# Nine late experts of 128 places, normed at a token's second visit, beside the tiles of the other tokens

## The chip, the core and the metric

One core of a Trainium2 chip. The time is that of the device for one execution of the whole kernel, in microseconds (us). PE is the matrix engine, DVE the vector engine, ACT the scalar engine, POOL the GpSimd engine (it also issues all DMAs with row lists), SP the engine that issues the weight loads.

## The reference, cut to what matters

One residual block over 2048 tokens of 1024 numbers. A mixer (convolution and gated DeltaNet) is added to x first. Then comes a mixture of experts, and the last norm:

```python
h = rms_norm(x, ffn_norm_g)
x = x + hier_moe(h, router_group_w, router_expert_w, w_gate, w_up, w_down)
return rms_norm(x, final_norm_g)
```

The router picks one of 4 groups for a token and 2 of the group's 8 experts; an expert is `(silu(x @ w_gate) * (x @ w_up)) @ w_down` with 1024, 512 and 1024 columns. So there are 4096 visits of a token to an expert, 32 experts, and a token's output row can be normed when both of its experts have been added.

On the inputs that the reference draws, the router sends between 85 and 173 tokens to an expert. With the experts ordered as the kernel does it, the last 3 get 300 visits by 288 tokens; the last 9 get 1002 visits by 842 tokens, of which 160 come twice; 1206 tokens come to none of the nine. The number of tokens whose first of two late visits is at the first, second, ... ninth late expert: 37, 40, 31, 0, 14, 26, 12, 0, 0.

## The kernel before, in words

Up to about 1060 us the mixer runs; then the block's sums x are written to `acc_d` in memory, and the normed halves of h to `h2_d`. Routing gives each expert a rank: ranks 0 to 2 are experts picked early, which had few tokens in the first half; the rest follow by falling number of tokens. `CAPS` (L725) gives each rank a number of places. Lists of token numbers, one per place, stand in `tabG` (for gathers, always a valid row), `tabS` (for scatters; an empty place points past the last row and is skipped) and `gix` (for the gates).

Each expert is one `Job` of one chunk (up to 128 places) or two. The loop at L1488 runs the 32 jobs; its first half (`gate_up`, 192 matmuls whose moving side has one column per place) and second half (`down`) are each woven by `weave` with other generators, which hand out the places in program order; from there the tile framework sets the order on each engine and the waits. For one job there are:
- `load_part` (L766, L775): 12 stages of 512 KB, loaded by SP into `mst` tiles, scaled and split into two f16 halves by ACT (`wgu`, `wd`, L92) and DVE (L93). `stage()` takes the tiles from two pools of five in turn. The split halves have two buffers each, so the next expert is loaded while one runs. SP's queue runs in order.
- `fetch` (L1050, L1055): POOL gathers the tokens' rows of h and their gates; `turn` (L1066, L1067) turns them on PE.
- `gate_up` (L1081 to L1088), then `down`. With one chunk, `down` makes 24 matmuls of 512 columns (L1116) and ACT scales by the gate (L1125). With two chunks, it makes 96 matmuls with one column per place (L1151), and PE turns the result back (L1138, L1142).
- `add` (L1094): POOL scatters the result onto `acc_d`, adding in memory, one DMA for each chunk.

The order of jobs (L1329 on) takes large and small ranks in turn: 2, 28, 3, 27, 4, 26, ..., 16, 15, and then the last three ranks, 29 to 31 (`LAST = 3`). All tiles of tokens are normed at the end: `others` (L1252) makes the list `bix`, by which a tile's tokens with a visit to the last three are left out. The first eight tiles are gathered into stages (`load_early`, L1378) when the last weights are through, the other eight (`load_late`) into a weight buffer after the last gathers. `norm_all` squares (L1366), takes the root (L1369, a power on POOL at L1370), applies the gain (L1373) and writes twelve tiles by SP as whole tiles (L1410) and four by lists on POOL (L1414). Rows of the late tokens are gathered once more (`rows_of`, L1421), normed (`norm_rows`) and scattered last (`store_rows`, L1432); the last expert's result is added to gathered sums on DVE (L1123) rather than in memory. `behind` and `issue_after` hold the norms back behind the experts' work. A loop for experts with more tokens than places follows; it runs no round on these inputs.

## Time and profile before

| what | us |
|---|---|
| median of 3 runs | 1954.14 (1949.02 to 1956.95) |
| the profiled execution | 1948.9 |
| its span | 1947.1 |
| PE busy | 1752.6 |
| DVE busy | 1403.5 |
| ACT busy | 1007.2 |
| POOL busy | 426.7 |

Times in the trace count from the start of the span. "Busy" of PE is modelled, as matmuls overlap. The DMA share is the mean over the core's 16 DMA engines of the time that packets took, so it can come out a little over 1. A `POOL DMA_INDIRECT` row is the time that POOL takes to issue a DMA with a row list; its data land later. In a timeline row the brackets name the idle time before the instruction and what ended it.

### The profile page before, as it was taken

To read this page: it belongs to the slowest core of one execution; us is meant where nothing else is said; L and a number is where in the kernel's file an instruction comes from. 1 tells how busy PE (TensorE), PEld (TensorE's weight loads), DVE (VectorE), ACT (ScalarE), POOL (GpSimd) and SP (SyncE) were. 2 spreads that over 40 slices of the span, in tenths; PEclk is the share of its full clock that TensorE was granted. 3 is DMA by queue.
4 is the path that set the end of the run, shared out by engine and by line. 5 is a ranking of instruction groups with operands and counts; after the bars stand their busy time and mean duration, and the time that the engine had idled before them with its cause. 6 is when DMAs were issued, how large, how long until landed. Compare 5 with 4: busy or idle time off the path is not lost.

```text
span 1947.1 us, 41829 instructions
## 1 busy us (share of the span) xinstructions
PE 1752.6 (90%) x16221; PEld 1199.0 (62%) x16221; DVE 1403.5 (72%) x2713; ACT 1007.2 (52%) x1676; POOL 426.7 (22%) x375
## 2 busy tenths in 40 slices
PE   6789999999999999999999969999899999999840
PEld 5455555555555554444454438888788899999730
DVE  8889888888888745322344768777778888888732
ACT  5655434444444424211233637766667767777621
POOL 1321111121111100000000013223322344344343
PEclk9889999999999999999999979999999999999975
DMA  4122001001001105002255967999999999999873
GB/s 143 67 69 53 11 15 46 16 13 46 20 11 37 36 19 165 28 12 60 98 175 189 346 233 258 334 308 306 303 320 359 354 335 340 351 341 317 285 225 142
DMA packets 203597, 330.27 MB, mean 170 GB/s; under 512 B 44590, under 2 KB 98935, under 8 KB 203394
## 3 DMA queue, kind: packets, MB, share of 16 engines
q1 hardware_dynamic: 178738, 271.20, 40.9%
q0 software_dynamic: 20128, 47.30, 9.5%
q10 hardware_dynamic: 4528, 9.06, 1.2%
q8 instruction: 129, 2.11, 0.4%
q14 instruction: 74, 0.61, 0.1%
HBM read 276.05 MB, written 54.82 MB: 170 GB/s over the span
## 4 chain that ended last, share of the span: by engine, by line
PE 29%; DMA 20%; DVE 8%; issue 5%; ACT 5%; POOL 1%; SPq 1%; ACTq 0%; DVEq 0%; POOLq 0%
PE acc L134 11%; DMA mst<-in_w_up_dram 10%; PE a L1081 8%; DMA mst<-in_w_down_dram 5%; PE a L988 5%; DMA mst<-in_w_gate_dram 3%; DVE wgu L93 3%; ACT wgu L92 2%; DVE wd L93 1%; PE pn L548 1%; DMA end<-acc_d,tabG 1%; ACT yo L1142 1%; DMA mst<-acc_d,bix 1%; PE pl L1138 1%; SPq L766 1%
## 5 line engine op out<-in xcount | busy, mean ns | idle before, releaser
L134 PE MATMUL acc<-hT,whl 128*128 128x512 f16 x2640 | 635.3, 381 | 0.2 <-DVE hT L203 0.2
L134 PEld LDWEIGHTS <-whl 128*128 128x128 f16 x2640 | 252.9, 99 | 248.4 <-issue 11.4
L1081 PE MATMUL a<-xT,wgu 128*128 128x128 f16 (+17 forms) x6144 | 394.7, 227 | 3.3 <-DVE sl L1088 2.4
L1081 PEld LDWEIGHTS <-wgu 128*128 128x128 f16 x6144 | 389.3, 99 | 9.5 <-issue 3.5
L93 DVE SCALAR_TENSOR_TENSOR wgu<-mst,gw,wgu 128x1024 f16<-128x1024 f32 x256 | 317.5, 1276 | 19.9 <-ACT wgu L92 17.6
L92 ACT ACTIVATE wgu<-mst,gw 128x1024 f16<-128x1024 f32 x256 | 280.8, 1139 | 36.0 <-DMA mst<-in_w_up_dram 33.7
L988 PE MATMUL a<-wo,yb 128*128 128x512 f16 x768 | 176.3, 381 | 0.0
L93 DVE SCALAR_TENSOR_TENSOR wd<-mst,wd 128x1024 f16<-128x1024 f32 x128 | 154.2, 1215 | 3.6 <-ACT wd L92 3.5
L1094 POOL DMA_INDIRECT acc_d<-yo,tabS x50 | 95.9, 1918 | 265.9 <-ACT yo L1142 191.8
L92 ACT ACTIVATE wd<-mst 128x1024 f16<-128x1024 f32 x128 | 131.3, 1047 | 24.3 <-DMA mst<-in_w_down_dram 24.1
L1151 PE MATMUL a<-ac,wd 128*128 128x144 f16 (+12 forms) x1824 | 136.9, 230 | 4.9 <-ACT ac L92 3.9
L1151 PEld LDWEIGHTS <-wd 128*128 128x128 f16 x1824 | 124.4, 98 | 8.3 <-issue 6.5
L988 PEld LDWEIGHTS <-yb 128*128 128x128 f16 x768 | 72.2, 98 | 79.6 <-issue 3.0
L294 DVE SCALAR_TENSOR_TENSOR cv<-raw,pcol,cv 128x512 f32<-128x512 f32 x144 | 117.1, 815 | 1.6
L1050 POOL DMA_INDIRECT xr<-h_d,tabG x51 | 61.5, 1206 | 179.2 <-PE t L1066 159.0
L1088 DVE SCALAR_TENSOR_TENSOR sl<-a,sl 128x128 f32<-128x128 f32 (+17 forms) x128 | 38.3, 300 | 78.1 <-ACT sl L1087 77.6
L1087 ACT ACTIVATE sl<-a 128x128 f32<-128x128 f32 (+17 forms) x128 | 35.7, 280 | 108.9 <-PE a L1081 108.9
L1116 PE MATMUL pl<-wd,ac 128*128 128x512 f16 (+4 forms) x312 | 78.6, 397 | 6.1 <-ACT ac L92 4.8
L382 DVE TENSOR_TENSOR pr<-Ts,fs 32x1 f32<-32x1 f32 (+14 forms) x240 | 76.6, 319 | 4.4 <-DMA fs<-dscr 0.7
L1055 POOL DMA_INDIRECT gs<-gt_d,gix x51 | 74.3, 1457 | 15.7 <-issue 15.4
L545 ACT ACTIVATE osq<-acv 128x512 f32<-128x512 f32 x16 | 10.1, 628 | 125.3 <-DVE acv L543 125.3
L1138 PE MATMUL pl<-id,yt 128*128 128x128 f32 (+13 forms) x304 | 52.8, 292 | 23.4 <-ACT yo L1142 17.2
(357 smaller groups left out, 2536.6 us busy)
## 6 DMA issues: line engine op xcount, KB each, us to landing
mst<-in_w_gate_dram SPq DMA_DIRECT2D x256, 256.0 KB
mst<-in_w_up_dram SPq DMA_DIRECT2D x256, 256.0 KB
mst<-in_w_down_dram SPq DMA_DIRECT2D x128, 512.0 KB
wst<-in_w_in_dram SPq DMA_DIRECT2D x28, 512.0 KB
xt<-in_x_dram SPq DMA_DIRECT2D x16, 512.0 KB
ydr<-yh SPq DMA_DIRECT2D x64, 128.0 KB
x<-in_x_dram SPq DMA_DIRECT2D x16, 512.0 KB
yb<-ydr SPq DMA_DIRECT2D x16, 512.0 KB
```

What stands on the lines that cost most here:

```text
L92: A.activation(hi, src, AF.Copy, scale=scale)
L93: (eng or V).scalar_tensor_tensor(lo, src, scale, hi, op0=OP.mult, op1=OP.subtract)
L134: T.matmul(acc, w[:, i, k, :], hT[b][:, j, k, :], start=(n == 0), stop=(n == 3 * KT - 1))
L294: V.scalar_tensor_tensor(y, tap(j), pcol[:, q:q + 1], y, op0=OP.mult, op1=OP.add)
L382: V.tensor_tensor(q, Ts[:, 0:i, 0:i].rearrange("p j m -> p m j"), bc(fs[:, None, 0:i, i], [32, i, i]), op=OP.mult)
L988: T.matmul(po, yb[:, i, k, c * P:(c + 1) * P], wo[:, j, k, n * FF:(n + 1) * FF], start=(q == 0), stop=(q == 3 * KT - 1))
L1055: G.indirect_dma_start(out=g[0:cw], out_offset=None, in_=gt_d[0:end * NE, :], in_offset=IO(ap=gx, axis=0))
L1081: T.matmul(pg[:, q, 0:n], wq[:, i, k, q, f * P:(f + 1) * P], xT[:, j, k, 0:n], start=(z == 0), stop=(z == 3 * KT - 1))
L1094: st = G.indirect_dma_start(out=acc_d, out_offset=IO(ap=sx, axis=0), in_=yo[0:cw], in_offset=None, bounds_check=S - 1, oob_is_err=False, c ...
L1116: T.matmul(py[0:n], ac[:, i, k, 0:n], wd[:, j, k, q * FF:(q + 1) * FF], start=(z == 0), stop=(z == 3 * FF // P - 1))
L1138: T.transpose(py[0:cw, c * P:(c + 1) * P], yts[d2][:, u, off:off + cw], id32)
L1151: T.matmul(pg[:, u, 0:n], wd[:, i, k, d * P:(d + 1) * P], ac[:, j, k, 0:n], start=(z == 0), stop=(z == 3 * FF // P - 1))
```

## The change

- `LAST` is 9, so ranks 23 to 31 come last, with 128 places each (112 for the last). The jobs before them are then rank 2 (128 places), 22 (128), 3 (216), 21 (136), 4 (192), 20 (136), 5 (176), 19 (136), 6 (176), 18 (136), 7 (168), 17 (136), 8 (160), 16 (144), 9 (160), 15 (144), 10 (152), 14 (144), 11 (152), 13 (144), 12 (152).
- Places are rounded up to multiples of 8, and gathers (`even`) to multiples of 16 rows.
- `others` and the new `visits` make two lists per late expert: `tabF` (tokens whose first of two late visits this is) and `tabL` (tokens whose last visit this is), through a table `fl_d` in memory.
- In each of the late jobs but the last, the sums of the job's tokens are gathered to `so` at the start of `down` (`sums_before`). Its result is scattered onto `acc_d` for the tokens of `tabF` alone (`first_sums`). In the next job DVE adds result and sums, and the rows are normed and scattered to the output by `tabL` (`second_sums`).
- In each of the first eight late jobs two tiles of the other tokens are gathered into two stages during `gate_up` and normed and scattered to the output by `bix` during `down` (`load_tiles`, `norm_tiles`); no tile is written by SP.
- The last job ends with its own norm and scatter alone. The tables of routing move into tiles that other tables have left.

```diff
-    CAPS = [C1, C1, C1, 216, 188, 176, 172, 164, 160, 156, 152, 148, 148, 144, 144, 144, 140, 136, 136, 136,
-            132, 132, 128, 128, 124, 124, 124, 120, 120, 120, 116, 112]
+    CAPS = [C1, C1, C1, 216, 192, 176, 176, 168, 160, 160, 152, 152, 152, 144, 144, 144, 144, 136, 136, 136,
+            136, 136, 128, 128, 128, 128, 128, 128, 128, 128, 128, 112]
-    LAST = 3
+    LAST = 9
...
+    def even(n):
+        return max(n, min(-(-n // 16) * 16, CM - P if n <= CM - P else P))
...
     def others():
-        pq = o1.tile([P, 2, NT, NE], F32, name="pq2", tag="hx", bufs=1)
-        V.tensor_tensor(pq, OH, bc(last[:, None, None, :], [P, 2, NT, NE]), op=OP.mult)
-        yield 1
-        m = o2.tile([P, 2, NT], F32, name="om", bufs=1)
-        V.tensor_reduce(m, pq, axis=AX, op=OP.add)
...
+        for i, row in ((0, last), (1, capE)):
+            pq = o1.tile([P, 2, NT, NE], F32, name="pq2", tag="hx", bufs=1)
+            V.tensor_tensor(pq, OH, bc(row[:, None, None, :], [P, 2, NT, NE]), op=OP.mult)
+            yield 1
+            V.tensor_reduce(m[:, i], pq, axis=AX, op=OP.add)
+            yield 1
...
+        V.scalar_tensor_tensor(fl[:, :, 0], m[:, 2, 0], -BIG, tok, op0=OP.mult, op1=OP.add)
+        V.scalar_tensor_tensor(fl[:, :, 1], m[:, 2, 1], BIG, tok, op0=OP.mult, op1=OP.add)
+        nc.gpsimd.dma_start(fl_d.rearrange("(t p) c -> p t c", p=P), fl)
...
+    def visits():
+        for l in range(LAST):
+            G.indirect_dma_start(out=flp[:, l], out_offset=None, in_=fl_d,
+                                 in_offset=IO(ap=tabG[:, NE - LAST + l, 0:1], axis=0))
+            yield 1
...
-    AHEAD = 8
-    LP, WE = 0, 0.6
-    GT = 4
-    NPL = NT - GT
+    GT = 2
...
+    def load_tiles(t0):
+        for t in range(t0, t0 + GT):
             xs[t] = stage()
-            load(t)
+            st = G.indirect_dma_start(out=xs[t], out_offset=None, in_=acc_d,
+                                      in_offset=IO(ap=bix[:, t:t + 1], axis=0), bounds_check=S - 1,
+                                      oob_is_err=False)
...
-    def load_late():
...
-    def norm_all():
...
+    def norm_tiles(t0):
+        s = o2.tile([P, GT], F32, name="ss4")
+        for i in range(GT):
+            square(xs[t0 + i], s[:, i:i + 1])
+            yield 1
+        root(s)
+        yield 1
+        for i in range(GT):
+            x = xs.pop(t0 + i)
+            gain(x, s[:, i:i + 1])
+            store_rows(x, bix[:, t0 + i:t0 + i + 1])
+            yield 1
...
-    def finish(J):
...
+    def first_sums(J, l):
+        st = G.indirect_dma_start(out=acc_d, out_offset=IO(ap=tabF[0:J.n, l:l + 1], axis=0),
+                                  in_=(J.base or J.yo)[0][0:J.n], in_offset=None, bounds_check=S - 1,
+                                  oob_is_err=False, compute_op=OP.bypass if J.base else OP.add)
...
+    def sums_before(J):
+        J.so = rows_of(J.chunks[0][0], J.n, m2.tile([P, D], F32, name="so", bufs=1))
+        yield 1
+
+    def second_sums(J, l):
+        n, x = J.n, J.so
+        V.tensor_tensor(x, x, J.yo[0][0:n], op=OP.add)
+        yield 1
+        s = o2.tile([P, 1], F32, name="ss1", bufs=4)[0:n]
+        square(x, s, n)
+        yield 1
+        root(s)
+        yield 1
+        gain(x, s, n)
+        store_rows(x, tabL[0:n, l:l + 1])
+        yield 1
...
+        if l > 0:
+            parts.append((second_sums(jobs[j - 1], l - 1), 4, 0.1, 0.6))
+        if tl is not None:
+            parts.append((load_tiles(tl), GT, 0.5, 0.7))
+        if left == 1:
             J.base = [rows_of(J.chunks[0][0], J.n, stage())]
-            ends = [(rows_of(L.chunks[0][0], L.n, o1.tile([P, D], F32, name="end", tag="hh")), L.chunks[0][2])
-                    for L in jobs[-LAST:-1]]
-            load_late()
...
+        parts = [(part(j + 2, 0), 4, 0, 1)]
+        if 0 <= l and left > 1:
+            parts.append((sums_before(J), 1, 0, 0.1))
+        if tl is not None:
+            parts.append((norm_tiles(tl), 2 * GT + 1, 0, 0.9))
...
     end = stage()[0:J.n]
-    def rest():
-        for x, sx in ends:
-            norm_rows(x)
-        yield from slices(na, 2 * GT)
-        norm_rows(J.base[0][0:J.n], end)
-        yield from slices(na, 2 * GT)
-        for x, sx in ends + [(end, J.chunks[0][2])]:
-            store_rows(x, sx)
-    drain(behind(rest(), marks[-1]))
+    norm_rows(J.base[0][0:J.n], end)
+    store_rows(end, tabL[0:J.n, LAST - 1:LAST])
+    drain(first_sums(J, LAST - 1))
```

## Rows read from the trace of the kernel before

**Rows 1.** Busy us (instructions) by stretch; last: PE clock, DMA share, GB/s.

```profile
core 0: us, PE busy (x) PEld busy (x) DVE busy (x) ACT busy (x) POOL busy (x), PEclk, DMA share, GB/s
1700.00:1800.00 100.00, 98.45 (x1532) 94.40 (x1530) 87.89 (x126) 76.19 (x111) 42.97 (x27) 1.00 1.02 332
...
1850.00:1900.00 50.00, 23.95 (x240) 16.46 (x240) 14.93 (x28) 14.91 (x35) 20.96 (x21) 0.77 0.75 231
1900.00:1947.00 47.00, 0.00 (x0) 0.00 (x0) 13.66 (x14) 7.87 (x16) 13.59 (x12) 0.50 0.36 135
```

**Rows 2.** Timeline of PE, first `gate_up` matmuls of jobs 4, 5, 6, 17, 23, 31.

```profile
1241.63 17.92 PE L1081 MATMUL a<-xT,wgu 128*128 128x216 f16 x192
...
1272.55 0.90 PE L1081 MATMUL a<-xT,wgu 128*128 128x120 f16 x14
...
1290.14 15.68 PE L1081 MATMUL a<-xT,wgu 128*128 128x188 f16 x192
...
1550.39 0.39 PE L1081 MATMUL a<-xT,wgu 128*128 128x132 f16 x4
...
1682.07 0.58 PE L1081 MATMUL a<-xT,wgu 128*128 128x136 f16 x7
...
1860.28 0.85 PE L1081 MATMUL a<-xT,wgu 128*128 128x112 f16 x14
```

**Rows 3.** POOL's groups, from 1600 us on: busy us, mean ns, idle before.

```profile
L1094 POOL DMA_INDIRECT acc_d<-yo,tabS x19 | 35.7, 1880 | 70.5 <-ACT yo L1142 67.4 <-ACT sl L1087 1.5 <-issue 0.9
L1055 POOL DMA_INDIRECT gs<-gt_d,gix x19 | 30.0, 1577 | 5.8 <-issue 5.8
L1050 POOL DMA_INDIRECT xr<-h_d,tabG x18 | 22.5, 1248 | 35.3 <-PE t L1066 35.3
...
L1378 POOL DMA_INDIRECT mst<-acc_d,bix x8 | 15.5, 1936 | 15.3 <-DMA mst<-in_w_down_dram 13.1 <-DVE wgu L93 0.6 <-issue 0.6
...
L1414 POOL DMA_INDIRECT out_dram<-xw,bix x4 | 5.8, 1452 | 2.5 <-DVE xw L1373 1.9 <-issue 0.6
L1370 POOL TENSOR_TENSOR ss<-ss,mhalf 128x4 f32<-128x4 f32 x4 | 5.0, 1247 | 9.0 <-DVE ss L1369 9.0
```

**Rows 4.** Two stretches of one us: weights alone; gates and adds beside them.

```profile
1663.00:1664.00 1.00, 1.00 (x19) 1.00 (x17) 1.00 (x2) 1.00 (x2) 1.00 (x1) 1.00 1.07 406
...
1690.00:1691.00 1.00, 1.00 (x21) 1.00 (x19) 1.00 (x3) 0.32 (x1) 1.00 (x1) 1.00 1.02 234
```

**Rows 5.** DMA of 1500 to 1600 us.

```profile
DMA packets 15583, 35.31 MB, mean 353 GB/s; under 512 B 2124, under 2 KB 2124, under 8 KB 15568
```

**Rows 6.** DVE's groups by shape, from 1600 us on.

```profile
L93 DVE SCALAR_TENSOR_TENSOR wgu<-mst,gw,wgu 128x1024 f16<-128x1024 f32 x72 | 89.6, 1275 | 0.0
L93 DVE SCALAR_TENSOR_TENSOR wd<-mst,wd 128x1024 f16<-128x1024 f32 x38 | 46.1, 1213 | 0.0
L1067 DVE COPY xT<-t 128x1024 f16<-128x1024 f16 x18 | 11.5, 680 | 0.0
...
L93 DVE SCALAR_TENSOR_TENSOR ac<-sl,ac 128x136 f16<-128x136 f32 x12 | 3.5, 293 | 1.1 <-ACT ac L92 1.1
...
L1373 DVE SCALAR_TENSOR_TENSOR mst<-mst,ss,gfin 128x1024 f32<-128x1024 f32 x8 | 10.0, 1277 | 5.2 <-POOL ss L1370 5.2
```

**Rows 7.** Timeline of POOL and DVE in the tail.

```profile
1865.40 2.17 POOL L1094 DMA_INDIRECT acc_d<-yo,tabS  x1 [8.81 <-ACT sl L1087]
...
1879.32 1.02 POOL L1421 DMA_INDIRECT mst<-acc_d,tabG  x1 [10.67 <-DMA acc_d<-yo,tabS]
...
1936.64 0.96 POOL L1432 DMA_INDIRECT out_dram<-mst,tabS  x1 [8.51 <-DMA out_dram<-end,tabS]
...
1887.18 1.41 DVE L1123 SCALAR_TENSOR_TENSOR mst<-pl,gs,mst 112x512 f32<-112x512 f32 x2 [11.43 <-DMA mst<-acc_d,tabG]
```

**Rows 8.** Us from issue to landing after 1800 us; SP's waits (sum, times, longest), 1600 to 1800.

```profile
mst<-acc_d,bix POOLq DMA_INDIRECT x8, 7.1
...
SPq L775 <- DVE wgu L93: 38.5, 11, 5.7
```

**Rows 9.** Timeline of POOL, a gather of a tile while DVE splits weights.

```profile
1840.44 6.60 POOL L1378 DMA_INDIRECT mst<-acc_d,bix  x1 [0.31 <-DVE wgu L93]
```

## What the change will do to the time

> **What bounds the kernel now.** I read the stretches first (busy time, granted clock and DMA by stage), then the matrix engine's starts by job, then what every engine does in one job, then the chain of waits at the end. The second part of the kernel runs 32 experts ("jobs"). In the steady part DMA is always busy and PE, DVE and ACT are at 98, 88 and 76 of 100 us; after the last weights have landed, DMA falls to a share of 0.36 and PE stands still with its clock at half [rows 1]. So there are two regimes: a middle where nothing has much room, and a tail of 86.8 us, from the start of the last job (1860.28) to the end of the span (1947.1), in which the sums of all tokens are read back, normed and written. The change takes work out of the tail and puts it into the full stretch; the question is what it costs there.
>
> What one job takes is seen where successive jobs start [rows 2]. The six two-chunk jobs from 1550.39 to 1682.07 took 131.7 us for 848 places, 21.95 each at 141.3 places. A place more costs 192 + 96 matmul columns, 0.12 us at the full clock of 2.4 GHz, so 21.3 us at 136 places; the job of 216 then comes to 30.9, and 30.92 is what it took (1241.63 to 1272.55). A one-chunk job has no transposes back and took 17.6 (to 1290.14): it leaves PE room, and there DMA sets the pace.
>
> **The middle.** Before, jobs 4 to 22 alternate large and small experts and took 440.4 us (1241.63 to 1682.07) [rows 2]. After, the small experts are kept for the end, and the same 19 jobs are all two-chunk, with 2960 places: 19 x 21.3 + (2960 - 2584) x 0.12 = 450 us by PE. DMA needs 6.29 MB of weights and 156 places x 8 KB, 7.6 MB in 23.7 us, 320 GB/s, under the 332 that a hundred steady microseconds held [rows 1]; so PE is the bound. The rounded places are in this sum (36 places here, 4.3 us); the extra rows that a gather brings for 16 (at most 8 a job) are DMA alone and hidden. In jobs 4 and 5 come the tables: the nine gathers of `visits` have no counterpart, the nearest is the gather of gates, 1.58 us of POOL each [rows 3], while the DMA rate falls from 406 to 234 GB/s in such stretches [rows 4]: 14 us x 0.42 = 6 us of DMA as the upper end, none as the lower, since those jobs are PE-bound. The store of 2048 eight-byte pieces and the DVE work of `others` lie beside a 31 us job. I take 4: the middle is 13.6 us longer. Ends: +9.6, and +21 with the 6 us and 1 us more in each of the five jobs of 136 places (7.4 MB at 332 GB/s is 22.3 us, not 21.3).
>
> **The nine late jobs.** Each of eight jobs gets: 128 sums gathered, two tiles gathered (1206 tokens in 16 tiles, so 151 rows), three norms, 151 rows and (from the second) some 94 scattered to the output; its scatter-add shrinks from some 110 rows to 18. What each resource needs for one such job:
> - DMA: 6.29 weights + 0.52 for tokens + 0.52 sums + 0.62 + 0.62 tiles + 0.38 second visits + 0.07 first sums = 9.02 MB. At 353 GB/s, the best hundred microseconds [rows 5], 25.6 us; at 332 [rows 1], 27.2. For the higher rate speaks that the add in memory, which runs where the rate is down at 234 [rows 4], is nearly gone.
> - DVE: 8 x 1.24 + 4 x 1.21 splits, 2 x 0.64, 8 x 0.29 (`ac`, and `sl` of the same shape), three gains at 1.25, an add (not shown before at this place; its operands are as large as the gain's, so 1.25, with 0.64, the copy of half the bytes, and 2.5, the gain twice, as ends), roots 0.3: 23.7 us, busy time by count [rows 6].
> - POOL, which also takes over the twelve tile stores that SP issues now: 1.25 + 1.58 for the fetch, 3 x 1.94 gathers of sums, 3 x 1.45 stores, 1.88 for the first sums, two powers at 1.25, and 0.3 between instructions: 20.7 us [rows 3].
> - PE 18; three squares go into ACT's room.
>
> So DMA sets 25.6 us; I take it, as the fraction of adds is the larger difference between the two rates. The first of them lacks the second visit: 24.4. Jobs 23 to 30 take 24.4 + 7 x 25.6 = 203.6, against 178.2 before (1682.07 to 1860.28) [rows 2]: 25.4 longer. Ends: 23.7 a job (DVE) and 30 (below). The PE clock may fall in the waits, as to 0.77 late now [rows 1]; with 18 of 25.6 us it has cover, and none if jobs became PE-bound.
>
> **The tail.** Now: the last job starts at 1860.28, the scatter-add before it is issued at 1865.40, the gather of its sums waits for that until 1879.32, DVE has them at 1887.18, and then come twelve more tiles, norms, and three scatters in a row to 1936.64 [rows 7]. After: the same chain without the tiles. The scatter-add of job 30 has no row left (no token of it has a later visit), so its landing is short: gather at about +11 from the job's start, landed at +18, as gate_up (192 x 112 columns at 2.4 GHz, 9.0) and 24 matmuls of 512 columns at 0.21 end at about +16 with their waits; two evictions 1.5, square, root, power, gain 4, issue and landing 5, and the end of the program 5 to 6, as after the last issue now [rows 7]. That is 34 us against 86.8: 52.8 shorter. Ends: 30, and 50 if the wait for the add stays as it is now (10.7 us) and the last second visit stands before the last norm on DVE and POOL.
>
> **The sum.** 13.6 + 25.4 - 52.8 = -13.8. The profiled execution took 1948.9 (span 1947.1), so 1935.1; it stands 5.2 under the median of 1954.1, so the forecast is 1940, 0.7% faster. About 0.5%, 9.8 us, is what a measurement of this kernel can tell from no change.
>
> **Rivals.**
> - **DMA is not the limit, DVE is.** Gathers of whole rows may run near the 406 GB/s of the weights [rows 4]; then a late job takes DVE's 23.7: 15 us less, 1925. For it: no add in memory. Against: every steady hundred microseconds stayed at 332 to 353. Chance 0.22.
> - **The stage buffers run out (slower).** The tiles are gathered into the ten stages through which the weights pass. A tile holds its stage from its gather (7.1 us to landing [rows 8]) over squares, power and gains to the landing of its store, some 21 us, while that buffer comes round again after 10 of 14 stages, 18 us. The next weight load is issued late, and all loads behind it on SP's queue with it, where SP already waits up to 5.7 us for stages [rows 8]. Behind it on ACT and DVE stands the split, and behind that the activations of the running expert. Price: nothing to 10 us a job; with the doubled weight buffers hiding a little over half, 4.4: 30 us a job, 1971. It decides against the change above 27.6 us a job, by over 0.5% above 29. Chance 0.20.
> - **POOL becomes the bound.** One gather of a tile took 6.60 us while DVE ran splits without a pause, where its like take 1.94 [rows 3, 9]. Eight of POOL's eleven instructions in a late job are such issues beside a DVE that is nearly full. If one and a half a job go that way, 7 us more: 27.7 a job, 1955. Chance 0.12. The Trainium skill (SBUF — State Buffer, section "Who interferes with whom") says that a DVE instruction with two inputs from SBUF contends with a GpSimd instruction that reads SBUF, under an exclusive lock, and so speaks against this change; the trace agrees in that one row, not in the others, and were it the rule each time, the sum would be this rival's.
> - **The tail does not shrink as meant**, 50 us for 34: 1956. Chance 0.06.
>
> **How the numbers follow.** The forecast has 0.40; its own range, 24.7 to 27 us a job, is 1932 to 1950. Of that 0.28 lies under 1944.4. Faster by over 0.5%: 0.28 + 0.22 = 0.50. Within 0.5%: 0.12 + 0.10 (POOL) + 0.05 (tail) = 0.27. Slower: 0.20 + 0.03 = 0.23. The range leaves out the lower part of the second case and the upper half of the stage rival: 1914 to 1972.
>
> **What would show it.** Job starts: nineteen jobs from 1241 to about 1696, eight about 25 us apart, the last at 1900, the end 34 us later. In the late stretch DMA share near 1.0 at about 350 GB/s, DVE over 90 of 100, POOL near 80. If the wait rows of SP show the landing of a store to the output or of a tile as releaser, with DMA share under 0.9, the stages were the limit. If POOL has no idle time and long issues, POOL was. If the middle is longer than 462, the reading that PE bounds it is wrong. Late jobs under 23 us would show DVE's sum as too large.

## The result, and the profile after

The changed kernel takes 1980.2 us (median of 4 runs, 1969.4 to 1981.2), the kernel before 1951.6 beside it: a ratio of 1.0133, 95% interval 1.0087 to 1.018. It is slower by 1.3%, where 0.7% faster was forecast, and lies above the range. The profiled execution of the change took 1981.2, its span is 1979.1, 32.0 longer than the 1947.1 of before.

First the timeline of PE: the first `gate_up` matmuls of jobs 1, 4, 23 and 31 in the changed kernel ([rows 2] for before).

```profile
1202.16 2.03 PE L1088 MATMUL a<-xT,wgu 128*128 128x128 f16 x29
...
1261.10 3.12 PE L1088 MATMUL a<-xT,wgu 128*128 128x216 f16 x32
...
1715.91 0.50 PE L1088 MATMUL a<-xT,wgu 128*128 128x128 f16 x6
...
1948.87 7.88 PE L1088 MATMUL a<-xT,wgu 128*128 128x112 f16 x157
```

The starts split the 32.0 us into the terms of the forecast:

| stretch | before | after | difference | forecast |
|---|---|---|---|---|
| up to job 4 | 1241.6 | 1261.1 | +19.5 | 0 |
| jobs 4 to 22 | 440.4 | 454.8 | +14.4 | +13.6 |
| jobs 23 to 30 | 178.2 | 233.0 | +54.8 | +25.4 |
| job 31 to the end | 86.8 | 30.2 | -56.6 | -52.8 |

Two terms hold. One of 19.5 us was not in the sum, and the late jobs take 29.1 us each (233.0 / 8) for 25.5 in the sum (203.6 / 8). The profiled execution is the slowest of the change's four, so the table splits 32.0 us, where the medians differ by 28.6. The tail is as described: POOL's and DVE's timeline of the changed kernel has the gather of the last sums, the add of the second half, and the last scatter (answering to [rows 7]).

```profile
1955.53 0.96 POOL L1448 DMA_INDIRECT mst<-acc_d,tabG  x1 [0.30 <-issue]
...
1968.50 0.97 POOL L1413 DMA_INDIRECT out_dram<-mst,tabL  x1 [1.61 <-DVEq L1558]
...
1964.13 0.75 DVE L1130 SCALAR_TENSOR_TENSOR mst<-pl,gs,mst 112x512 f32<-112x512 f32 x1 [1.84 <-PE pl L1123]
```

Now the stretches of the changed kernel, to be held against [rows 1] (busy time of each engine, PE clock, DMA share, GB/s).

```profile
core 0: us, PE busy (x) PEld busy (x) DVE busy (x) ACT busy (x) POOL busy (x), PEclk, DMA share, GB/s
1700.00:1800.00 100.00, 74.23 (x919) 59.53 (x917) 66.84 (x90) 60.76 (x92) 45.12 (x33) 0.88 0.84 271
1850.00:1900.00 50.00, 35.39 (x383) 24.38 (x384) 35.27 (x46) 33.05 (x48) 19.37 (x15) 0.83 0.90 312
1950.00:1979.00 29.00, 13.83 (x197) 11.32 (x194) 9.36 (x17) 4.32 (x12) 9.48 (x9) 0.80 0.21 67
```

In the late stretch nothing is full: DMA has a share of 0.84 to 0.90 at 271 to 312 GB/s, DVE 67 of 100, POOL 45. So neither the forecast's limit nor that of the rivals on DVE and POOL was reached; the time is in waits. The view of waits of the changed kernel, 1745 to 1945 (sum, times, longest):

```profile
POOL so L1448 <- DMA out_dram<-so,tabL: 43.4, 7, 7.8
...
ACT wgu L92 <- DMA mst<-in_w_up_dram: 25.4, 23, 3.5
ACT wd L92 <- DMA mst<-in_w_down_dram: 21.8, 13, 3.8
PE a L1088 <- DVE sl L1095: 19.2, 6, 8.9
...
DVE mst L1410 <- POOL ss L1407: 14.0, 6, 7.3
...
SPq L776 <- DMA out_dram<-mst,bix: 58.1, 6, 14.0
...
SPq L767 <- DMA out_dram<-mst,bix: 5.3, 1, 5.3
```

SP waits 63 us until a tile's scatter to the output has landed and a stage is free, and ACT 47 us for the weights that come late; [rows 8] had at most 5.7 us at a time, for a stage that DVE was still splitting. That is the row named ahead for the stage rival, with its 30 us a job. But POOL waits too. How one wait can make the next is seen in one timeline, from the second half of job 24 into job 25 (POOL, DVE, SP, PE, in this order); of the eight late jobs it is the one with the longest waits before the power and the gain:

```profile
1765.61 0.94 POOL L1448 DMA_INDIRECT so<-acc_d,tabG  x1 [4.39 <-DMA out_dram<-so,tabL]
1774.75 1.61 POOL L1460 DMA_INDIRECT acc_d<-yo,tabF  x1 [8.20 <-DMA so<-acc_d,tabG]
1775.83 1.29 POOL L1407 TENSOR_TENSOR ss<-ss,mhalf 128x2 f32<-128x2 f32 x1
...
1782.02 2.03 POOL L1413 DMA_INDIRECT out_dram<-mst,bix  x1 [0.30 <-DVE wgu L93]
...
1768.48 0.16 DVE L1406 TENSOR_SCALAR ss<-ss 128x2 f32<-128x2 f32 x1
...
1777.15 2.48 DVE L1410 SCALAR_TENSOR_TENSOR mst<-mst,ss,gfin 128x1024 f32<-128x1024 f32 x2 [7.33 <-POOL ss L1407]
...
1769.95 17.28 SPq L776 DMA_DIRECT2D mst<-in_w_down_dram  x4
...
1784.62 5.29 PE L1088 MATMUL a<-xT,wgu 128*128 128x128 f16 x48 [8.91 <-DVE sl L1095]
```

Read from the top: the gather of the sums before waits for the only `so` buffer (4.39). The scatter-add of the first sums, on the same memory, waits for that gather to land (8.20). Behind both on POOL stands the power for the two tiles, whose input DVE had ready at 1768.48; it issues at 1775.83. So DVE stands 7.33 before the tiles' gain, with splits and the running expert's `sl` behind it, and PE 8.91. The tiles' scatter leaves at 1782; their gathers had been issued at 1751.50 and 1752.85, so a tile holds its stage 31 us up to the issue of its scatter alone, and SP's four loads spread over 17.28. The Trainium skill (PSUM — Partial Sum Buffer, section "Engine vs sequencer instructions") calls the queues of ScalarE, VectorE and GpSimdE strict FIFO; the trace agrees, with 7 us between the power's input and its issue.

This chain is not the whole of it. Only for three of the eight pairs of tiles does the power stand behind the scatter-add (7.2, 2.3 and 2.3 us after its input was ready); for the other five it is issued within 0.5 us of its input. What all eight have in common lies before it, on DVE: from the end of a pair's second square on ACT to the first instruction of its root on DVE it is 4.1 to 11.9 us, in which DVE works through splits that stand ahead, or waits for ACT's part of them; that lengthens the hold of the stages. For the pair of job 26:

```profile
1821.60 0.18 ACT L1403 ACTIVATION_READ_ACCUMULATOR jk<-mst 128x1 f32 x1
...
1833.63 0.16 DVE L1406 TENSOR_SCALAR ss<-ss 128x2 f32<-128x2 f32 x1
```

### The profile page after: what moved, and what is told of

Read it like the earlier page. It is cut to its first block, busy times and chain, and to the rows that moved or that the text cites. A ratio compares the mean times of both kernels' runs of the same rounds, so it can differ in the third digit from the quotient of the medians.

```text
span 1979.1 us, 41955 instructions
## 1 busy us (share of the span) xinstructions
PE 1782.5 (90%) x16221; PEld 1204.5 (61%) x16221; DVE 1424.4 (72%) x2748; ACT 1016.0 (51%) x1688; POOL 501.7 (25%) x412
## 5 line engine op out<-in xcount | busy, mean ns | idle before, releaser
L1088 PE MATMUL a<-xT,wgu 128*128 128x128 f16 (+9 forms) x6144 | 406.4, 229 | 26.0 <-DVE sl L1095 19.2
L1088 PEld LDWEIGHTS <-wgu 128*128 128x128 f16 x6144 | 398.7, 99 | 35.9 <-issue 20.6
L1101 POOL DMA_INDIRECT acc_d<-yo,tabS x42 | 111.2, 2648 | 194.8 <-ACT yo L1149 160.7
L1123 PE MATMUL pl<-wd,ac 128*128 128x512 f16 (+1 forms) x312 | 98.6, 471 | 52.4 <-ACT ac L92 41.4
L1158 PE MATMUL a<-ac,wd 128*128 128x136 f16 (+7 forms) x1824 | 138.7, 231 | 0.2 <-issue 0.2
L1094 ACT ACTIVATE sl<-a 128x128 f32<-128x128 f32 (+9 forms) x128 | 36.1, 282 | 125.2 <-PE a L1088 76.8
L1095 DVE SCALAR_TENSOR_TENSOR sl<-a,sl 128x128 f32<-128x128 f32 (+9 forms) x128 | 38.6, 302 | 83.9 <-ACT sl L1094 71.5
L1123 PEld LDWEIGHTS <-ac 128*128 128x128 f16 (+1 forms) x312 | 33.7, 117 | 105.6 <-ACT ac L92 52.3
L93 DVE SCALAR_TENSOR_TENSOR ac<-sl,ac 128x128 f16<-128x128 f32 (+9 forms) x128 | 38.9, 304 | 60.3 <-ACT ac L92 53.1
L304 POOL TENSOR_TENSOR zr<-zr,sg 128x512 f32<-128x512 f32 x16 | 24.3, 1520 | 208.1 <-ACT sg L302 201.2
```

The source lines that it names most:

```text
L93: (eng or V).scalar_tensor_tensor(lo, src, scale, hi, op0=OP.mult, op1=OP.subtract)
L1088: T.matmul(pg[:, q, 0:n], wq[:, i, k, q, f * P:(f + 1) * P], xT[:, j, k, 0:n], start=(z == 0), stop=(z == 3 * KT - 1))
L1095: V.scalar_tensor_tensor(sl[:, 0:n], pg[:, 1, 0:n], ACS / WS, sl[:, 0:n], op0=OP.mult, op1=OP.mult)
L1101: st = G.indirect_dma_start(out=acc_d, out_offset=IO(ap=sx, axis=0), in_=yo[0:cw], in_offset=None, bounds_check=S - 1, oob_is_err=False, c ...
L1123: T.matmul(py[0:n], ac[:, i, k, 0:n], wd[:, j, k, q * FF:(q + 1) * FF], start=(z == 0), stop=(z == 3 * FF // P - 1))
L1158: T.matmul(pg[:, u, 0:n], wd[:, i, k, d * P:(d + 1) * P], ac[:, j, k, 0:n], start=(z == 0), stop=(z == 3 * FF // P - 1))
```

## The experiments

The theories: (A) **stages**: tiles stand in the ring of the weights; (B) **order**: the tile's square, power and gain stand in queues behind waits that are not theirs; (C) **work**: bytes or instructions; and for the early loss (D) the marks of the visits, nine gathers and their readers. "Late job" is the start of job 31 less that of job 23, by eight. Ratios are to the kernel before, on the same chip.

**Runs 1 to 4.** The first leaves out the lines that load and norm tiles, the second those of the second visits.

```diff
-            parts.append((load_tiles(tl), GT, 0.5, 0.7))
-            parts.append((norm_tiles(tl), 2 * GT + 1, 0, 0.9))
```

> Leaves out the tiles of the other tokens in the late jobs: their two gathers, two squares, power, two gains and two scatters to the output; the rows of these 1206 tokens aren't written. The changed kernel's late job took 29.1 us (1715.91 to 1948.87 over eight) in a program of 1980. If the stages are the cause (a tile keeps the stage that the next weight load wants until its scatter has landed, and SP's queue waits with it), the row of SP waiting for the tiles' scatter is gone and a late job takes 25 us: 1980 - 8 x 4 = 1948. If the single buffer of the sums before (their gather waits for the last scatter of the same buffer, with POOL's later work behind it) is the cause, that wait stays and a job takes 28 to 29 us: 1970 to 1980. If DMA bytes are the limit, a job falls by the 1.24 MB of the tiles at 310 GB/s, 4 us: 1948 as well, so this run sorts out only the second theory; the one with tiles in buffers of their own sorts out the third.

```diff
-            parts.append((second_sums(jobs[j - 1], l - 1), 4, 0.1, 0.6))
-            parts.append((sums_before(J), 1, 0, 0.1))
```

> Leaves out the second visits of the late jobs (gather of the sums before, add, square, power, gain, scatter to the output); the rows of tokens whose last visit is in the first eight of the nine late jobs aren't written. If the stages are the cause, SP's waits for the tiles' scatters stay and a late job takes 27 to 28 us: 1964 to 1972. If the single buffer of the sums before is the cause, a job takes 25 to 26 us: 1948 to 1956. If DMA bytes are the limit, 0.9 MB at 310 GB/s less, 2.9 us a job: 1957.

The third (`mst` and `mst2` go from five to four buffers each) and the fourth:

```diff
-            xs[t] = stage()
+            xs[t] = m2.tile([P, D], F32, name="xt", bufs=GT)
```

> The whole computation, with the tiles in two buffers of their own, taken from the stages: weights pass through 8 stages for 10 throughout. If the stages are the cause because tiles stand in their ring, SP's waits for a scatter to the output are gone and a late job takes 26 us: 1980 - 8 x 3 = 1956, less what eight stages cost in the middle (0 to 10 us more). If the number of stages at hand is what matters, not who holds them, nothing is won: 1980 to 1990. If DMA bytes or the single buffer of the sums before are the cause: 1980, and SP's wait rows alone change.

```diff
-            parts.append((seq(ovf, others()), 16, 0, 1))
+            parts.append((behind(seq(ovf, others()), latest()), 16, 0, 1))
-            parts.append((visits(), LAST + 1, 0.2, 1))
+            parts.append((behind(visits(), latest()), LAST + 1, 0.2, 1))
```

> The whole computation, with the lists (the marks of each token's visits, their store, the nine gathers) held behind the work of the job in whose place they are written, as the kernel before does with its norms. In the changed kernel they ran in job 0 and gate_up of job 1 began 17.3 us later than in the kernel before (1202.16 against 1184.94). If the lists at that place are the cause, job 1 begins at 1185 and job 4 at 1242, and the program takes 1980 - 17 = 1963, or 1967 if the nine gathers cost 4 us in jobs 4 and 5. If the early gap has another cause (the gathers' lists wait that is ahead of them on POOL for the fetch of job 2, which stands in both kernels), job 1 still begins near 1202: 1980.

| run | us | ratio (95%) | late job |
|---|---|---|---|
| no tiles | 1910.4 | 0.980 (0.9756 to 0.9844) | 21.0 |
| no second visits | 1944.3 | 0.9995 (0.9978 to 1.0013) | 25.2 |
| tiles in own buffers | 1995.3 | 1.0257 (1.0232 to 1.0282) | 31.3 |
| lists held | 1971.8 | 1.0125 (1.0101 to 1.0148) | 29.4 |

Both halves cost, the tiles 8.1 us a job, twice what any theory gave them. Buffers of their own make it worse: SP's waits for scatters are gone, and ACT stands instead until the tiles have landed. The waits of the second run and of the third:

```profile
ACT jk L1403 <- DMA mst<-acc_d,bix: 46.6, 13, 8.2
```

```profile
ACT jk L1403 <- DMA xt<-acc_d,bix: 61.8, 16, 10.6
```

So (A) alone falls: the wait moves with the buffer. That the weights have eight stages there for ten is no cause of its own: run 11 has eight too, with late jobs of 25.6 us. With the lists held, job 2 begins at 1196.6 (before 1197.4, after 1214.7), but job 5 then takes 32.3 us for 22.1, where DVE stands for the ninth gather. That wait is in the first run's job 1 too. The waits of the first run and of the fourth:

```profile
DVE flp L1291 <- DMA flp<-fl_d,tabG: 11.3, 1, 11.3
```

```profile
DVE flp L1291 <- DMA flp<-fl_d,tabG: 10.2, 1, 10.2
```

**Runs 5 to 8.** Neither tiles nor second visits (all four lines of the first two diffs out):

> Leaves out both the tiles and the second visits of the late jobs (the rows of 1206 tokens and of those whose last visit is in the first eight late jobs aren't written). Late jobs took 29.1 us with both, 25.2 without the second visits, 21.0 without the tiles. If the two costs simply add (each takes its share of a full resource), a late job takes 29.1 - 3.9 - 8.1 = 17.1 us. If they hurt because they meet in the queues that run in order (the tile's square waits on ACT, the stage's next load on SP, the power on POOL, behind each other), what is left with neither is the job's own work, set by ten or twelve weight loads, DVE and PE: 19 to 20.5 us, and second visits alone cost only some 1 us a job. Time 1890 to 1905.

A late job takes 17.5 us (1882.8 in all; 0.9649, 0.9627 to 0.967). The costs add, as the first case has it: 17.1 expected (the whole time is below the 1890 to 1905 that was given). The stretch of that run, in the columns of the stretches above:

```profile
1710.00:1850.00 140.00, 136.86 (x1871) 110.93 (x1870) 129.73 (x171) 113.53 (x170) 47.70 (x20) 1.00 0.96 343
```

PE and DMA are both full, so what is added must be paid for at least in bytes. As an estimate, a late job moves 6.0 MB here, 6.8 without tiles (325 GB/s over the late jobs), 7.3 without second visits (290) and 8.2 in the changed kernel (281); at 343 GB/s that is 19.9, 21.3 and 23.9 us for the last three. The run without tiles is 1.1 above that, the one without second visits 3.9, the changed kernel 5.2. So the second visits cost little more than their bytes, and most of what was not foreseen sits with the tiles.

The marks' readers three jobs later:

```diff
+        elif j == 8:
+            parts.append((behind(marks_of(), latest()), 1, 0.2, 1))
```

> The whole computation. The nine gathers of the marks stay where they are; only the four short instructions of DVE that read them, 128 x 9 each, are moved to three jobs later and held there. In the traces of the runs without tiles and without second visits the first of them stood on DVE for 10.9 to 11.3 us in job 1 until the ninth gather had landed, with the split and the running expert's activations behind it. If that wait is the early loss, job 2 begins at 1198 to 1202 instead of 1208 to 1215, and the program takes 1980 - 10 = 1970. If POOL is the cause (nine gathers ahead of the fetch of job 2 and of the scatter-add), job 2 or job 3 is as late as before: 1978 to 1980.

1977.5 us (1.0142, 1.0118 to 1.0165); job 2 begins 44.6 us after job 0 (after 48.5, without tiles 41.6, before 31.6). The expected gain failed: DVE's wait is gone, and the fetch of job 2 still stands behind nine gathers on POOL, at 1189.

Twelve tiles in the late jobs and four in the last:

```diff
+    TS = [range(a, b) for a, b in ((0, 1), (1, 3), (3, 4), (4, 6), (6, 7), (7, 9), (9, 10), (10, 12), (12, 16))]
```

> The whole computation, with one or two tiles in each of the eight late jobs (12 in all, for 16) and four in the last job, which loads no weights, so that its stages are free. If a tile in a late job costs by the wait for its stage and in the queues, the four moved ones cost nothing to 6 us in the last job and their share, 8.1 / 2 = 4 us each, is saved: 1980 - 16 + 3 = 1967; more, to 1955, if a job with one tile gets by without any wait. If the cost belongs to the second visits meeting a job without room, whatever the number of tiles, late jobs stay at 28 to 29 us and the last one grows: 1980 to 1985.

1978.1 us (1.0137, 1.012 to 1.0154): a late job takes 27.7, but job 31 and the end take 44.3 for 30.2. A tile costs 14.1 / 4 = 3.5 us there and 8.1 / 2 = 4.0 in a late job, so moving four wins nothing. Then other places within the same job:

```diff
-            parts.append((load_tiles(tl), GT, 0.5, 0.7))
+            parts.append((load_tiles(tl), GT, 0.8, 0.95))
-            parts.append((norm_tiles(tl), 2 * GT + 1, 0, 0.9))
+            parts.append((norm_tiles(tl), 2 * GT + 1, 0.3, 0.7))
```

> The whole computation, with other places for the same instructions: tiles gathered at 0.8 to 0.95 of gate_up (before: 0.5 to 0.7), their norms at 0.3 to 0.7 of down (before: 0 to 0.9). The stage is held shorter and the square comes to ACT later after its gather. If it is the time that a tile holds its stage, and squares that come too early, a late job falls from 29.1 to 26 to 27.5 us: 1955 to 1967. If it is the work as such (DMA bytes, the instructions of DVE and POOL): 1978 to 1982. If POOL's order is what decides (gathers and powers behind the wait for the second visit's store), the tiles' gathers come later still and a job is as long or longer: 1980 to 1995.

1985.6 us (1.0165, 1.0143 to 1.0188), 30.0 a late job: no better, as the third case has it. ACT now waits 36.7 us for tiles to land. In neither of the two placements does the chain of gather, square, power, gain and scatter fit into its half job.

**Runs 9 to 11.** The lists once more, with both waits out (the edits of the fourth and the sixth run together):

> The whole computation. The lists are held behind the jobs in whose place they are written, and the four instructions of DVE that read the nine gathers come three jobs after them. Each alone left about 10 us: with the lists held, job 2 began at 1196.6 as in the kernel before, but job 5 took 32.3 us for 22 (DVE stood 10.2 us for the ninth gather); with the readers moved alone, the fetch of job 2 still stood behind the nine gathers on POOL (issued at 1189 for 1180) and job 2 began at 1207. If these two waits are the whole early loss, and each covers the other when it is taken away alone, both go here: job 5 takes 22 to 23 us, job 23 begins at 1695 to 1698 (1715.9 in the changed kernel, 1706.6 with the lists held), and the program takes 1961 to 1965. If POOL's fifteen busy microseconds in job 5 cost by themselves (the next fetch and the scatter-add behind them), job 5 takes 27 or more: 1967 to 1972.

1976.4 us (1.0129, 1.0106 to 1.0152); job 5 takes 28.4 and job 23 begins at 1709.3: the second case by its job 5 (27 or more), and later than its 1967 to 1972. Then the order of the tiles, in buffers of their own, and in the next run that of the sums:

```diff
+        if 0 < l and GT * (l - 1) < NT:
+            parts.append((norm_tiles(GT * (l - 1)), 2 * GT + 1, 0.15, 0.7))
-            parts.append((load_tiles(tl), GT, 0.5, 0.7))
-            parts.append((norm_tiles(tl), 2 * GT + 1, 0, 0.9))
+            parts.append((load_tiles(tl), GT, 0.5, 0.75))
```

(the new `load_tiles` line stands in the second half of the job, the norms in the first half of the next)

> The whole computation. As in the run with tiles in two buffers of their own (8 stages for weights; late jobs of 31.3 us, ACT standing 61.8 us for tiles to land), but the tiles are gathered at 0.5 to 0.75 of down and normed in gate_up of the job after, at 0.15 to 0.7. Tiles hold no stage, and their square comes to ACT some 10 us after the gather. If the tiles cost by those two waits (SP's for the stage, or ACT's for the landing), both are gone and a late job falls to what its bytes take, 24.5 to 26 us: 1980 - 8 x 3.5 = 1945 to 1955. If eight stages are the limit in late jobs, or the two buffers of the tiles come round too late (POOL's gather then waits for their scatter), 28 to 31 us: 1975 to 1995. If DVE and ACT are full in gate_up, where the norms now lie, PE waits there instead, and a job takes 27 to 28: 1962 to 1970.

```diff
-            parts.append((second_sums(jobs[j - 1], l - 1), 4, 0.1, 0.6))
+            parts.append((second_sums(jobs[j - 1], l - 1), 4, 0, 0.45))
-            parts.append((sums_before(J), 1, 0, 0.1))
+            parts.append((sums_before(J), 1, 0.35, 0.45))
```

> The same, and the gather of the sums before is moved from 0 to 0.1 of down to 0.35 to 0.45, their norm from 0.1 to 0.6 of the next gate_up to 0 to 0.45. In the changed kernel POOL stood 43.4 us in seven waits before that gather, until the last scatter from the one buffer had landed. If that wait on POOL costs time through what stands behind it (the power of the tiles, their scatters, the scatter-add), a late job is 1 to 2 us shorter than in the run with this order unmoved: 8 to 16 us less. If the wait is hidden (nothing behind it is urgent once the tiles are normed in the next job), no difference; if the sums now land too late for DVE's add, the next gate_up has DVE standing, and a job is 1 to 2 us longer.

1983.0 us (1.0161, 1.0136 to 1.0187) with 29.2 a late job, and 1957.8 (1.0033, 1.0017 to 1.005) with 25.6. In the first, ACT still stands 31.2 us for tiles; in the second 10.2. The move of the sums gains 25 us here for the 8 to 16 expected. Here the late stretch is what the forecast had, for the first time. Which of the three moves does it is what the last runs settle.

**Runs 12 to 16: early loss, and the sums alone.** In run 12 (all of this, and the marks spread out; 1959.9, 1.0048, 1.003 to 1.0066) and run 13 the nine gathers were not moved in fact: the trace has them in job 0, since only ACT's and DVE's instructions held them.

> The changed kernel with nothing moved but the marks: one gather in each of jobs 5 to 13, the readers in job 17. If the two waits (POOL nine gathers long, DVE behind the ninth) are the early loss: job 2 at 1198, job 4 at 1243 to 1245, job 23 at 1698 to 1702 (1715.9 in the changed kernel), late jobs of 29 us as before, 1980 - 15 = 1965 to 1969. If not: 1975 to 1980.

1980.8 us (1.0135, 1.0112 to 1.0157): no gain, as in the sixth run; with the gathers still in job 0 this does not decide between the cases. The sums moved alone (the last diff above, in the changed kernel):

> The changed kernel with nothing moved but the sums before: gathered at 0.35 to 0.45 of down (0 to 0.1), added and normed at 0 to 0.45 of the next gate_up (0.1 to 0.6). With tiles in buffers of their own and normed a job later, this same move took a late job from 29.2 to 25.6 us. If the wait of POOL before that gather is what costs most in the changed kernel too, a late job falls to 26 to 27: 1956 to 1964. If there the stage and the square's place decide first (SP's six waits of 9 us for a tile's scatter, ACT behind a tile that hasn't landed), late jobs stay at 28 to 29.5: 1972 to 1983; then only the moves together pay.

1994.5 us (1.0221, 1.0197 to 1.0246), 31.0 a late job: worse than either case; the move alone harms. ACT stands 46.1 us for tiles that have not landed (1715 to 1915; 3.6 in 200 us of the changed kernel); the wait comes up at another place of the chain. Then the marks, one gather a job:

```diff
-            parts.append((visits(), LAST + 1, 0.2, 1))
+        elif 5 <= j < 5 + LAST:
+            parts.append((behind(slices(vis, 1), latest(A, V, G)), 1, 0.2, 0.4))
```

> The changed kernel with the marks alone moved: in the run before this one the nine gathers still ran in job 0 (1181 to 1192), since only ACT's and DVE's instructions held them, and only their readers had moved; now POOL's own instructions hold each gather in its job, one in each of jobs 5 to 13, readers in job 17. If nine gathers in a row on POOL, ahead of the fetch of job 2, are the early loss: the fetch of job 2 is issued at 1180 instead of 1194.7, job 2 begins at 1198, job 4 at 1242 to 1245, job 23 at 1698 to 1703 (1715.9 in the changed kernel), late jobs stay at 29 us: 1980 - 15 = 1963 to 1968. If a gather costs wherever it stands (the next fetch and the scatter-add behind it), the gain is given back in jobs 5 to 13, 1 us in each: 1973 to 1978.

1979.1 us (1.0148, 1.0124 to 1.0172), past the end of the second case. The two waits are gone: the fetch of job 2 in the changed kernel, and then in this run (POOL's timeline):

```profile
1191.62 0.94 POOL L1287 DMA_INDIRECT flp<-fl_d,tabG  x1 [0.30 <-issue]
1194.73 0.94 POOL L1056 DMA_INDIRECT xr<-h_d,tabG  x1 [2.17 <-remote]
```

```profile
1182.08 0.99 POOL L1056 DMA_INDIRECT xr<-h_d,tabG  x1 [6.96 <-PE t L1073]
```

Job 2 begins at 1199.6 for 1214.7, but jobs 5 to 13 take 225.2 us for 216.4, one more each: a gather a job costs what nine in a row cost. (The edit also holds each gather behind other work of its job; the gather and the hold are not told apart.)

> The whole computation with all moves that paid: tiles in two buffers of their own and normed in the next job, the sums before gathered later, and one gather of the marks in each of jobs 5 to 13. The first three alone took 1957.8 with late jobs of 25.6 us. If the early loss is won too, and the two are independent: job 2 near 1198, job 23 near 1698, late jobs of 25.6 to 26 us, 1943 to 1949, below the kernel before (1952). If the gain is given back in jobs 5 to 13: 1953 to 1960.

1958.0 us (1.0026, 1.0013 to 1.0039): the late jobs take 25.8, and nothing is added by the marks, the second case.

**Runs 17 and 18: order without buffers.** The two order edits of runs 10 and 11 with the tiles in the stages, and then the edit of the tiles alone.

> The order of the run that brought late jobs to 25.6 us (tiles normed in the next job, sums before gathered later), but with the tiles in the ten stages of the weights again, as the change has them. A tile then holds its stage from 0.5 of down to 0.7 of the next gate_up and until its scatter has landed, longer than in the changed kernel. If the stages are a cause of their own, SP waits 50 us or more for the tiles' scatters again and a late job takes 28 to 31 us: 1975 to 1995. If only the places of the norms and sums in the queues of ACT and POOL mattered, a late job takes 25.5 to 26.5 as with buffers of their own: 1955 to 1962.

> The changed kernel with the tiles alone moved (gathered at 0.5 to 0.75 of down, normed in the next job's gate_up at 0.15 to 0.7, still in the weights' stages); the sums before stay at 0 to 0.1 of down and 0.1 to 0.6 of gate_up. Late jobs took 29.1 us in the changed kernel, 31.0 with the sums moved alone, 25.8 with both. If the tiles' square coming too early to ACT is the whole cause and the sums' move only keeps POOL's queue in step, this run has 26 to 27.5 us: 1950 to 1963. If POOL's wait before the gather of the sums (one buffer, the last scatter from it not landed) holds the tiles' gathers and powers behind it as much as before, a late job takes 28 to 29.5: 1970 to 1983, and only the two moves together pay.

1945.5 us (0.9961, 0.9943 to 0.9978) with 25.8 a late job, and 1946.1 beside a kernel before of 1944.8 (1.0003, 0.9992 to 1.0013) with 25.7. In both, the case in which the order decides came out, with times below the ones given for it. The first is the fastest whole kernel of the study: 0.4% faster than before, under the 0.5% that was named as no change, but against 1.3% slower for the change as made. In the late jobs the sums' move adds nothing once the tiles are moved and stand in the stages (in buffers of their own it was worth 3.6 us a job, runs 10 and 11; why it differs is not shown); whether the 0.4% between the two ratios is its doing or the chip's is not settled. The waits of the last run, 1715 to 1915, against those of the changed kernel in as long a stretch:

```profile
ACT jk L1403 <- DMA mst<-acc_d,bix: 25.6, 7, 10.3
...
ACT wgu L92 <- DMA mst<-in_w_up_dram: 10.4, 14, 5.4
...
DVE mst L1410 <- POOL ss L1407: 4.7, 6, 1.0
...
POOL so L1448 <- DMA out_dram<-so,tabL: 3.9, 3, 1.7
...
SPq L767 <- DMA out_dram<-mst,bix: 23.1, 6, 4.9
```

SP's 63 us are 23, ACT's 47 are 10, DVE's 14 are 4.7, and POOL's 43.4 are 3.9, though the sums were not touched. Not every wait falls: ACT's for tiles to land rises to 25.6 from 3.6, and SP stands about 110 us in all for 120, now mostly until DVE has split a stage. The granted clock makes no difference between the two (0.86 here, 0.83 there). POOL's timeline of that run shows the new order: powers first, then the tiles' scatters, then the sums' gather, and the scatter-add last.

```profile
1767.96 0.57 POOL L1407 TENSOR_TENSOR ss<-ss,mhalf 128x1 f32<-128x1 f32 x1 [4.74 <-DVE ss L1406]
1769.01 1.67 POOL L1407 TENSOR_TENSOR ss<-ss,mhalf 128x2 f32<-128x2 f32 x1 [0.48 <-DVE ss L1406]
...
1779.58 0.97 POOL L1448 DMA_INDIRECT so<-acc_d,tabG  x1 [0.30 <-issue]
...
1786.95 1.59 POOL L1460 DMA_INDIRECT acc_d<-yo,tabF  x1 [3.82 <-ACT yo L1132]
```

The tiles gathered at 1776.87 and 1780.85 leave at 1798.16 and 1804.08: they hold a stage 21 to 23 us instead of 31, although their norm was placed a job later; over all late jobs it is 21 to 27 us here, and 27 to 33 in the changed kernel but for its first and last pair. The wait on DVE between a pair's second square and its root is gone too, with 0.0 to 1.1 us for the eight pairs:

```profile
1794.60 0.19 ACT L1403 ACTIVATION_READ_ACCUMULATOR jk<-mst 128x1 f32 x1
...
1795.24 0.17 DVE L1406 TENSOR_SCALAR ss<-ss 128x2 f32<-128x2 f32 x1
```

(The two squares of a pair now lie 11 to 15 us apart, for 2 to 9, as they were placed.) So the places of the tiles' gathers and norms are what costs the 3.4 us a job. Which of the queues they stand in, ACT's, DVE's or POOL's, is the head of the chain is not shown: no run changes one of them alone. And in jobs 26 to 29 DMA is now the limit (stretches of that run):

```profile
core 0: us, PE busy (x) PEld busy (x) DVE busy (x) ACT busy (x) POOL busy (x), PEclk, DMA share, GB/s
1750.00:1800.00 50.00, 41.13 (x464) 30.03 (x465) 39.94 (x51) 34.97 (x55) 28.67 (x20) 0.83 0.96 338
1800.00:1850.00 50.00, 38.16 (x459) 29.38 (x457) 41.71 (x54) 35.54 (x54) 24.13 (x20) 0.86 0.97 351
```

## Why the prediction was wrong, point by point

- **The middle**: right. 454.8 us for 454 forecast. It is 451.7 to 456.0 in the eleven runs that do not touch the lists, so PE's count of columns (450) was good to 2 to 6 us; what makes the difference between them is open. The rounding of places alone was not tried.
- **The late jobs: the step that failed is "So DMA sets 25.6 us".** The bound itself was sound: in jobs 26 to 29 of run 18 a job moves 9.0 to 9.2 MB (9.02 in the sum) in 25.9 to 27.3 us at a DMA share of 0.96 to 0.97. That the mean comes out at 25.6 to 26.1 us a job in five runs with another order (runs 11, 12 and 16 to 18; 205.6 us in all in run 18, for 203.6) is in part luck, since the first two late jobs and the last move less, and the share over all eight is 0.90 at 311 GB/s. What failed is that a bound from sums of work was taken for the time, with nothing for the places of the norms in the queues. In the change a pair of tiles stands 4 to 12 us on DVE before its root and in three jobs of eight 2 to 7 us on POOL behind the scatter-add, holds its stages about 30 us, and the weights come late. With the norms a job later the wait on DVE is at most 1.1 us, the holds are 21 to 27, and the weights' lateness is 10 us for 47: 3.4 us a job, 27 in all (233.0 less 205.6). How the 27 us divide among the waits was not measured.
- **The stage rival** (0.20, 30 us a job, 1971) came out in its size and in the wait that it named. But it took the hold of a tile as 21 us and the ring as too short for that; the hold was 27 to 33 in most jobs. With 21 to 27 us SP's waits for tiles' scatters are 23 us for 63 and the ring of ten stages does, while stages saved without a new order (run 3) save nothing. So the order decides; the wait for stages is one way in which it reaches the weights.
- **DVE, POOL**: DVE's 23.7 us of work a job was 21.4 (147.21 busy in the 200 us from 1745, so 0.736 x 29.1), POOL's 20.7 was 14.1 (96.75 there). The POOL groups of the changed kernel, 1720 to 1900, answer to [rows 3, 9]:

```profile
L1425 POOL DMA_INDIRECT mst<-acc_d,bix x13 | 17.9, 1378 | 8.1 <-issue 7.5 <-DVE mst L1410 0.3 <-DMA mst<-in_w_down_dram 0.3
```

In these rows a tile's gather issues in 1.38 us on the mean; the 6.60 of before was a single case. The lock of which the Trainium skill tells (SBUF — State Buffer, section "Who interferes with whom") is one between a DVE instruction with two inputs from SBUF and a GpSimd instruction that reads SBUF. The trace agrees in part: of the 65 issues on POOL in the eight late jobs, the 19 with under a tenth of their time beside such instructions took 1.09 us on the mean, the 31 with over nine tenths 1.80, and all 16 above 1.9 us are among these 31; but others among them took 1.03 to 1.2. So whether it is the lock is not shown. Two gathers of a tile, the first with no such instruction beside it, the second wholly beside them:

```profile
1730.94 1.00 POOL L1425 DMA_INDIRECT mst<-acc_d,bix  x1 [0.30 <-issue]
...
1779.66 2.06 POOL L1425 DMA_INDIRECT mst<-acc_d,bix  x1 [0.30 <-DVE mst L1410]
```

The rival falls by its size: 0.7 us an issue, with POOL idle half the time.

- **The early loss: "the store of 2048 eight-byte pieces and the DVE work of `others` lie beside a 31 us job", and 4 us for nine gathers.** The lists are written into jobs 4 and 5, but nothing ties them there, and they ran in job 0. From job 0 to job 4 the kernel takes 75.9 us before, 94.9 in the profiled execution of the change, and 86.3 to 91.0 in eleven kernels that leave this part alone: 10 to 15 us as a rule, 19 in that one. With the lists held out of it (run 4) it is 79.0. Two waits were found, DVE behind the ninth gather and the fetch of job 2 behind all nine on POOL; taken away, separately or together, they come back as one us in each job or as 6 to 10 in job 5. From job 0 to job 23 it is 541 to 549 us in the four kernels with the gathers held (runs 4, 9, 15 and 16) and 538 to 545 in those eleven; before 516, to which the middle without lists adds 11 to 16 (451.7 to 456.0 less 440.4). So they cost some 10 us or more in both places. Why one gather of 8 bytes a row costs a full us of a job was not found.
- **The tail**: right, 30.2 us for 34, at the forecast's lower end; the last gather came at +6.7 instead of +11.

## What to carry to other kernels

A bound from sums of work holds only if each piece finds its queue free when its turn comes. Before a chain that crosses four engines and two DMAs is put beside a full stretch, ask for each in-order queue what stands directly ahead of it there and how long that waits, and give the chain a whole iteration between gather and norm: that one move, with the tiles in the stages, was worth 27 us, where buffers of its own were worth less than nothing. The longest wait in the list (here SP's, for a stage) can be the end of a chain and not its head; the timeline, read from the instruction that is ready but not issued, shows what is ahead of it. Read all iterations: here one alone would have put the whole loss on POOL, and the wait that all eight share was on DVE.

## What was not expected of the hardware

- With the order mended, row gathers, scatters and weight loads together ran at 338 and 351 GB/s with a share of 0.96 and 0.97, as fast as weights with the adds in memory before [rows 1, 5].
- Issues on POOL of DMAs with row lists took 1.80 us on the mean (1.03 to 2.63) beside DVE's instructions with two inputs in SBUF, and 1.09 us without, in the late jobs of the changed kernel.
- A gather of 128 rows of 8 bytes occupies POOL for about 0.94 us at a free queue, but with one held in each of jobs 5 to 13 these took 1.0 us more each (run 15 against the changed kernel) and 1.1 (run 16 against run 11, 226.5 for 216.2). The cause is open.
